# A two-layer decoder's expert layer: experts ranked by token count, the four emptiest with 64 slots and two matmul passes

## The chip, the core and the metric

The kernel runs on one NeuronCore of a Trainium2 chip. The metric is device time in microseconds (us), the median of several runs. The engines are TensorE (PE: matmuls; PEld: its weight loads), VectorE (DVE), ScalarE (ACT), GpSimd (POOL) and SyncE (SP, which here issues the weight transfers). Each engine works through its own list of instructions in order.

## The reference, cut to what matters

256 tokens of width 1024 pass two hybrid layers. Layer 1 ends in a mixture of eight expert SwiGLUs (inner width 2816), each token going to two of them:

```
logits = x @ w_router                       # 256 x 8
top_logit, top_idx = top_k(logits, 2);  top_w = softmax(top_logit)
out[t] = sum over the two experts e of token t:
         top_w * ( (silu(x[t] @ w_gate[e]) * (x[t] @ w_up[e])) @ w_down[e] )
x = layernorm(alpha * x + out)
```

For these inputs experts 0 to 7 get 52, 107, 68, 61, 52, 26, 119 and 27 of the 512 assignments.

## The kernel before, in words

**Weights.** All weights lie in one array `wst` as units of 128 x 2048 float32 (1.05 MB). `fetch` (L178) starts one transfer a unit from SP into a ring of buffers `raw`; in the expert layer one buffer `ga` is part of the ring too. Float32 precision comes from splitting each number: each half unit (128 x 1024) is rounded by ACT to `hi` (L197), and DVE computes `lo = raw - hi` (L199). A product is then three matmuls on 128 x 512 pieces (`mm3`: hi x hi L209, hi x lo L210, lo x hi L211).

**Expert layer** (`moe`). For each expert e, a `gather` (L1004, L1005: matmuls with a one-hot matrix `ohm`) packs its tokens into 128 slots: `xeh` and `xel`, the high and low parts of the packed tokens. Gathers are made for two experts at a time, in steps 3 to 6 of the odd expert before. Then come 11 steps j (`NJ`), 256 inner columns each, with three units a step, six halves (called a to f below; a to d are gate and up, e and f down):

1. gate and up: 24 matmuls into one bank `pa` (128 slots x 256 gate | 256 up);
2. ACT takes silu of the gate half (`fs`, L1095), DVE multiplies by the up half (L1096), PE transposes (L1101), ACT rounds to `hh` (L1105), DVE makes `hl2` (L1106);
3. down: 12 matmuls into two banks `Y`. They are held back (`pend`) and issued amid the gate and up matmuls of step j+1.

After step 10, `scatter` rounds `Y` to `yh` (ACT, L1052) and `yl` (DVE, L1053), brings the rows back to token order by eight matmuls (L1056, L1057), and DVE adds them, weighted, to the sum `ybc` (L222). For an expert this falls into the first steps of the next one.

**Overflow.** `weights`, in step 1 of expert 0, counts tokens per expert and keeps the largest count (`mosti`). `spill`, at expert 4 step 5 (`SPILL`), loads it into a register of every engine (L1121) and branches (`tc.If`, L1136) round a slow path for experts with over 128 tokens. With these inputs the branch is not entered.

The order of instructions on each engine is fixed when the kernel is built: a scheduler places them by the order of the code and by when tiles come free.

Of the kernel before, what the change touches and what calls it, by code (L numbers as in the profile page):

```python
# [45 lines left out]
SPILL = 4, 5  # L46
GA = 3
SPLITS = 3, 4, 3, 2, 3
# [87 lines left out]
class Net:  # L136
# [29 lines left out]
    def fetch(self):  # L166
# [12 lines left out]
        self.unit += 1  # L179
        return raw  # L180
# [21 lines left out]
    def halves(self):  # L202
        raw = self.fetch()
        for h in range(2):
            yield self.split(raw[:, h * 1024:(h + 1) * 1024])
# [708 lines left out]
    def route_consts(self):  # L914
        nc, C = self.nc, self.cst
        self.rt = C.tile([128, 8, NE], F32, name="rt")
        nc.gpsimd.dma_start(self.rt, self.A["router"])
        it = C.tile([128, 128], I32, name="it")
        nc.gpsimd.iota(it, pattern=[[1, 128]], base=0, channel_multiplier=0)
        self.io8 = C.tile([128, NE], F32, name="io8")  # L920
        nc.vector.tensor_copy(self.io8, it[:, 0:NE])
        self.slot = C.tile([128, 128], F32, name="slot")
        nc.vector.tensor_scalar(self.slot, it, 1.0, None, op0=OP.add)
        self.ones = C.tile([128, 128], F32, name="ones")
        nc.vector.memset(self.ones, 1.0)
# [8 lines left out]
        self.xkh = self.xkl = None  # L934

# [27 lines left out]
    def weights(self):  # L963
# [4 lines left out]
        most = C.tile([128, 1], F32, name="most")  # L968
        nc.vector.tensor_reduce(most, ps[:, 0:NE], axis=AX.X, op=OP.max)
        self.most = C.tile([128, 1], I32, name="mosti")  # L970
        nc.vector.tensor_copy(self.most, most)
        ex = C.tile([128, 2, 2], F32, name="ex")
        for m in range(2):
            nc.vector.tensor_scalar(ex[:, m], self.top[:, m, 0:2], self.top[:, m, 0:1], None, op0=OP.subtract)
        nc.scalar.activation(ex, ex, AF.Exp)
        den = C.tile([128, 2], F32, name="den")
        nc.vector.tensor_add(den, ex[:, :, 0], ex[:, :, 1])
        nc.vector.reciprocal(den, den)
        for m in range(2):
            nc.vector.tensor_scalar(ex[:, m], ex[:, m], den[:, m:m + 1], None, op0=OP.mult)  # L980
            nc.vector.tensor_scalar(self.wt[:, m], self.oh8[:, m, 0], ex[:, m, 0:1], None, op0=OP.mult)
            self.stt(self.wt[:, m], self.oh8[:, m, 1], ex[:, m, 1:2], self.wt[:, m])
        self.dump("pos", self.pos)
        self.dump("wt", self.wt)

    def gather(self, es, W):
        nc = self.nc
        n = len(es)
        oh = W.tile([128, 2, n * 128], F32R, name="ohm", bufs=2)
        self.front = []  # L990
        for m in range(2):
            for i, e in enumerate(es):
                self.front.append(nc.vector.tensor_scalar(oh[:, m, i * 128:(i + 1) * 128], self.slot,
                                                          self.pos[:, m, e:e + 1], None, op0=OP.is_equal))
        xeh = [W.tile([128, 8, 128], F32R, name="xeh", bufs=3) for _ in es]
        xel = [W.tile([128, 8, 128], F32R, name="xel", bufs=3) for _ in es]
        for kp in range(4):
            ps = self.pa()
            for kk in range(2):
                k = 2 * kp + kk  # L1000
                s = slice(k * 128, (k + 1) * 128)
                o = ps[:, kk * 256:kk * 256 + n * 128]
                for m in range(2):
                    nc.tensor.matmul(o, lhsT=self.xkh[:, m, s], rhs=oh[:, m], start=m == 0, stop=False)  # L1004
                    nc.tensor.matmul(o, lhsT=self.xkl[:, m, s], rhs=oh[:, m], start=False, stop=m == 1)  # L1005
            pv = ps.rearrange("p (k i t) -> p k i t", k=2, t=128)
            for i in range(n):
                q = slice(2 * kp, 2 * kp + 2)
                nc.scalar.copy(xeh[i][:, q], pv[:, :, i])
                self.front.append(nc.vector.tensor_sub(xel[i][:, q], pv[:, :, i], xeh[i][:, q]))  # L1010
            yield
        return [xeh, xel, oh]
# [8 lines left out]
    def turn(self, oh, W):  # L1021
        nc = self.nc
        oht = W.tile([128, 2, T], F32R, name="oht", bufs=2)
        for i in range(2):
# [5 lines left out]

    def moe(self, W):
        nc = self.nc
        acc = self.macc
        got = coming = None
# [3 lines left out]
        pend = None  # L1038

        def down(j, hh, hl2, wd, Y, ns=(0, 1)):  # L1040
            for f in range(2):
                for n in ns:
                    s = slice(n * 512, (n + 1) * 512)
                    self.mm3(Y[n], hh[:, f], hl2[:, f], wd[f][0][:, s], wd[f][1][:, s], j == 0 and f == 0,
                             j == NJ - 1 and f == 1)

        def scatter(e, Y, oht, ns=(0, 1)):
            for n in ns:
# [5 lines left out]
                for m in range(2):  # L1054
# [3 lines left out]
                    self.stt(acc[:, m, s], ps, self.wt[:, m, e:e + 1], acc[:, m, s])  # L1058

        for e in range(NE):  # L1060
            if e % 2 == 0:
                got = self.finish(coming or self.gather((e, e + 1), W))
                coming = None
                if e == 0:
                    self.after(SPLITS[1], self.front[SPLITS[4]])
            Y = oht = None
            for j in range(NJ):
                if e == 0 and j == 1:
                    self.weights()
# [4 lines left out]
                if e % 2 and e < NE - 1 and GA <= j < GA + 4:  # L1074
                    if coming is None:
                        coming = self.gather((e + 1, e + 2), W)
                    next(coming, None)
                if j == 2:
                    if e % 2 == 0:
                        got[2] = self.turn(got[2], W)  # L1080
                    oht = got[2][:, e % 2]
                ps = self.pa()
                for u in range(2):
                    raw = self.fetch()
                    for h in range(2):
                        hi, lo = self.split(raw[:, h * 1024:(h + 1) * 1024])
                        for kk in range(2):
                            k = 4 * u + 2 * h + kk
                            s = slice(kk * 512, (kk + 1) * 512)
                            self.mm3(ps, got[0][e % 2][:, k], got[1][e % 2][:, k], hi[:, s], lo[:, s], k == 0, k == 7)  # L1090
                        if u == 1 and h == 0 and pend is not None and not (e == NE - 1 and j == NJ - 1):
                            pend()
                            pend = None
                sg = W.tile([128, 256], F32, name="fs", bufs=2)
                nc.scalar.activation(sg, ps[:, 0:256], AF.Silu)  # L1095
                nc.vector.tensor_mul(sg, sg, ps[:, 256:512])  # L1096
                wd = list(self.halves())
                last = e == NE - 1 and j == NJ - 1
                pt = self.pb()
                for f in range(2):  # L1100
                    nc.tensor.transpose(pt[:, f * 128:(f + 1) * 128], sg[:, f * 128:(f + 1) * 128], self.ident)  # L1101
                hh = W.tile([128, 2, 128], F32R, name="hh", bufs=2)
                hl2 = W.tile([128, 2, 128], F32R, name="hl2", bufs=2)
                pv = pt[:, 0:256].rearrange("p (a t) -> p a t", a=2)
                nc.scalar.copy(hh, pv)  # L1105
                nc.vector.tensor_sub(hl2, pv, hh)  # L1106
# [4 lines left out]
                def pend(ns=(0, 1), j=j, hh=hh, hl2=hl2, wd=wd, Y=Y, e=e, oht=oht):  # L1111
                    down(j, hh, hl2, wd, Y, ns)
                    if j == NJ - 1:
                        scatter(e, Y, oht, ns)
        for n in range(2):
            before((n,))
            pend((n,))

    def spill(self, W, base):
# [16 lines left out]
        with tc.If(most > 128):  # L1136
            nc.vector.tensor_scalar(pos, self.pos, -128.0, None, op0=OP.add)
# [134 lines left out]
```

## Time and profile before

| | us |
|---|---|
| median of 3 runs | 1595.93 (1594.56 to 1597.03) |
| span of the profiled execution | 1596.8 |
| PE busy | 1525.8 (96%) |
| DVE busy | 1275.7 (80%) |
| ACT busy | 933.8 (58%) |
| last silu (L1095) starts | 1576.03 |

The profiled execution's own time is its span, 1596.8 us, 0.9 us over the median. Of the span, 0 to about 770 us are the mixers, the dense layer and the router, about 770 to 1586 us the expert layer, and the rest is the last layernorm and the output. A matmul's bar in the trace is longer than the distance to the next one, because matmuls overlap: a 128 x 512 matmul shows 0.40 us, and the next starts 0.23 to 0.24 us later. In a table by stretches the columns are the stretch, its length, the busy time of each engine with the number of its instructions, the granted clock of TensorE (1.00 is full), the busy share of the DMA engines, and GB/s.

### The profile page before, as it was taken

What the parts mean: (1) busy time and instruction counts of PE and PEld (TensorE: products, weight loads), DVE (VectorE), ACT (ScalarE), POOL (GpSimd) and SP (SyncE); (2) the same over time, 40 slices, a digit from 0 to 9 for tenths busy, and PEclk for the clock granted to TensorE, in tenths of its full rate; (3) what the DMA queues carried; (4) which work ended last, traced back from release to release, by engine and by line L of the source; (5) the groups of instructions that cost most, each with busy time, mean ns of one, the idle gap of its engine ahead of it and who ended that gap; (6) DMA issues with size and microseconds to landing.
All of it is one profiled execution on the core that took longest, in us unless ns stands there. A gap on an engine that the chain in (4) does not pass through costs nothing. (4 is left out here: it accounts for less than half of the span.)

```text
span 1596.8 us, 23711 instructions
## 1 busy us (share of the span) xinstructions
PE 1525.8 (96%) x9398; PEld 1316.9 (82%) x9398; DVE 1275.7 (80%) x1717; ACT 933.8 (58%) x1235; POOL 44.3 (3%) x80
## 2 busy tenths in 40 slices
PE   7989999999989989999899999999997999999996
PEld 7989988999979989898787887878875888788785
DVE  6899578655555898578898988888887888888887
ACT  6432454544426432455777777776775777767674
POOL 1020000000000210000000000000000000000000
PEclk9999999999999999999899999999998999999998
DMA  6343236555414333254897998989987988899892
GB/s 228 127 151 120 93 139 244 218 205 185 172 67 148 124 136 111 101 206 194 306 353 316 369 343 309 367 324 344 346 311 269 375 341 328 315 362 362 326 370 86
DMA packets 55636, 390.76 MB, mean 245 GB/s; under 512 B 6192, under 2 KB 6192, under 8 KB 9568
## 3 DMA queue, kind: packets, MB, share of 16 engines
q1 hardware_dynamic: 53136, 381.18, 63.4%
q0 software_dynamic: 2096, 7.49, 1.3%
q8 instruction: 75, 1.23, 0.3%
q10 hardware_dynamic: 288, 0.52, 0.1%
q14 instruction: 41, 0.34, 0.1%
HBM read 387.08 MB, written 2.10 MB: 244 GB/s over the span
## 5 line engine op out<-in xcount | busy, mean ns | idle before, releaser
L199 DVE TENSOR_TENSOR lo<-raw,hi 128x1024 fp32r<-128x1024 f32 x648 | 771.3, 1222 | 156.7 <-ACT hi L197 154.0
L197 ACT CAST hi<-raw 128x1024 fp32r<-128x1024 f32 x648 | 656.9, 1050 | 299.9 <-PE pa L210 185.3
L209 PE MATMUL pa<-xTh,hi 128*128 128x256 f32 x1120 | 325.4, 291 | 7.3 <-ACT xTh L348 7.3
L211 PE MATMUL pa<-xTh,lo 128*128 128x256 f32 x1120 | 323.9, 289 | 7.5 <-DVE lo L199 7.3
L210 PE MATMUL pa<-xTl,hi 128*128 128x256 f32 x1120 | 321.9, 287 | 2.3 <-DVE xTl L349 2.0
L211 PE MATMUL pa<-hi,xel 128*128 128x512 f32 x704 | 283.5, 403 | 0.0
L210 PE MATMUL pa<-lo,xeh 128*128 128x512 f32 x704 | 280.9, 399 | 1.2 <-DVE lo L199 1.2
L209 PE MATMUL pa<-hi,xeh 128*128 128x512 f32 x704 | 281.3, 400 | 0.4 <-ACT oht L1028 0.4
L209 PEld LDWEIGHTS pa<-xTh,hi 128*128 128x128 f32 x1120 | 218.7, 195 | 12.0 <-ACT xTh L348 7.3
L211 PEld LDWEIGHTS pa<-xTh,lo 128*128 128x128 f32 x1120 | 218.8, 196 | 11.5 <-DVE lo L199 10.1
L210 PEld LDWEIGHTS pa<-xTl,hi 128*128 128x128 f32 x1120 | 218.6, 195 | 3.6 <-DVE xTl L349 2.3
L209 PE MATMUL pb<-hi,hh 128*128 128x512 f32 x440 | 175.5, 399 | 8.9 <-PEq L1136 5.9
L210 PE MATMUL pb<-lo,hh 128*128 128x512 f32 x440 | 174.7, 397 | 0.0
L211 PE MATMUL pb<-hi,hl 128*128 128x512 f32 x440 | 173.8, 397 | 0.0
L210 PEld LDWEIGHTS pa<-lo,xeh 128*128 128x128 f32 x704 | 133.4, 190 | 32.1 <-DVE lo L199 1.9
L211 PEld LDWEIGHTS pa<-hi,xel 128*128 128x128 f32 x704 | 133.3, 189 | 29.3
L209 PEld LDWEIGHTS pa<-hi,xeh 128*128 128x128 f32 x704 | 133.4, 189 | 29.2 <-ACT oht L1028 0.6
L1095 ACT ACTIVATE fs<-pa 128x256 f32<-128x256 f32 x88 | 33.8, 384 | 138.4 <-PE pa L211 138.4
L209 PEld LDWEIGHTS pb<-hi,hh 128*128 128x128 f32 x440 | 83.2, 189 | 29.6 <-issue 6.1
L211 PEld LDWEIGHTS pb<-hi,hl 128*128 128x128 f32 x440 | 83.3, 189 | 20.2 <-DVE hl L1106 0.2
L210 PEld LDWEIGHTS pb<-lo,hh 128*128 128x128 f32 x440 | 83.2, 189 | 19.4
L199 DVE TENSOR_TENSOR lo<-ga,hi 128x1024 fp32r<-128x1024 f32 x74 | 88.1, 1219 | 8.0 <-ACT hi L197 7.6
(329 smaller groups left out, 1538.3 us busy)
## 6 DMA issues: line engine op xcount, KB each, us to landing
raw<-in_wst SPq DMA_DIRECT2D x322, 1024.0 KB, 6.2
ga<-in_wst SPq DMA_DIRECT2D x37, 1024.0 KB, 6.8
raw<-in_wst SPq DMA_DIRECT2D x4, 512.0 KB, 5.7
xf<-in_xT SPq DMA_DIRECT2D x2, 512.0 KB, 5.6
raw<-in_lora SPq DMA_DIRECT2D x2, 512.0 KB, 5.7
kk<-in_lnp POOLq DMA_DIRECT2D x2, 512.0 KB, 3.8
v<-in_lnp POOLq DMA_DIRECT2D x2, 512.0 KB, 3.7
xsave<-ga POOLq DMA_DIRECT2D x2, 512.0 KB, 2.9
```

The source lines that it names most:

```text
L197: self.nc.scalar.copy(hi, src)
L199: self.nc.vector.tensor_sub(lo, src, hi)
L209: mm(out, lhsT=lh, rhs=rh, start=start, stop=False)
L210: mm(out, lhsT=lh, rhs=rl, start=False, stop=False)
L211: mm(out, lhsT=ll, rhs=rh, start=False, stop=stop)
L1095: nc.scalar.activation(sg, ps[:, 0:256], AF.Silu)
```

## The change

The eight counts are ranked on the chip; rank 0 is always expert 0 (work on it begins before the counts are known), ranks 1 to 7 follow by falling count. The weight transfers of ranks 1 to 7 take their address from a register of SP. Ranks 0 to 3 run as before with 128 slots. Ranks 4 to 7 get 64 slots. Their packed tokens hold the high parts in columns 0 to 63 and the low parts in columns 64 to 127 of one 128 x 128 operand, so that two passes (`mm2`: times `hi`, times `lo`) do what three did; rows 0 to 63 and 64 to 127 of the result then have to be added. In `hidden_small` ACT copies the gate and up bank to `gu`, four float32 matmuls with `fold` (two identities on top of each other) add the two halves and transpose at once, ACT takes silu, DVE multiplies, and ACT and DVE write the high and low parts of `hh` side by side. Gathers are made for rank groups (0), (1, 2), (3), (4, 5), (6, 7). The branch of `spill` moves behind the last scatter, and its condition is now that any expert has more tokens than its slots (128 or 64).

```
-SPILL = 4, 5
-SPLITS = 3, 4, 3, 2, 3
+SPLITS = 3, 4, 3, 2, 1
+BIG = 4
+GROUPS = (0,), (1, 2), (3,), (4, 5), (6, 7)
+LIMITS = 128, 64
...
-        w = self.A["wst"][self.unit]
+        w = self.A["wst"][self.unit] if src is None else src
...
+    def rank(self, cnt, W):                    # on DVE, small tiles, 128 x 8 or 128 x 64
+        self.stt(key, cnt, float(NE), self.tie)
+        nc.vector.tensor_tensor(sq, key[:, None, :].to_broadcast([128, NE, NE]),
+                                key[:, :, None].to_broadcast([128, NE, NE]), op=OP.is_gt)
+        nc.vector.tensor_reduce(rk, sq, axis=AX.X, op=OP.add)
...
+        self.permute(self.posr, self.pos, W)
...
+    def expert_unit(self, r, j, c):
+        if r == 0:
+            return None
+        if r not in self.who:
+            self.who[r] = self.nc.values_load(self.order[0:1, r:r + 1], engines=(mybir.EngineType.SP,),
+                                              min_val=0, max_val=NE - 1)
+        src = self.A["wst"][bass.ds(self.who[r] * (3 * NJ) + (self.base + 3 * j + c), 1)]
...
+    def mm2(self, out, l, rh, rl, start, stop):
+        self.nc.tensor.matmul(out, lhsT=l, rhs=rh, start=start, stop=False)
+        self.nc.tensor.matmul(out, lhsT=l, rhs=rl, start=False, stop=stop)
...
+        def hidden_small(ps):
+            gu = W.tile([128, 512], F32, name="gu", bufs=2)
+            nc.scalar.copy(gu, ps)
+            pt = self.pb()
+            for f in range(4):
+                nc.tensor.matmul(pt[:, f * 64:(f + 1) * 64], lhsT=gu[:, f * 128:(f + 1) * 128], rhs=self.fold,
+                                 start=True, stop=True)
+            sg = W.tile([128, 2, 64], F32, name="fs", bufs=2)
+            pv = pt[:, 0:256].rearrange("p (a t) -> p a t", a=4)
+            nc.scalar.activation(sg, pv[:, 0:2], AF.Silu)
+            nc.vector.tensor_mul(sg, sg, pv[:, 2:4])
+            hh = W.tile([128, 2, 128], F32R, name="hh", bufs=2)
+            nc.scalar.copy(hh[:, :, 0:64], sg)
+            nc.vector.tensor_sub(hh[:, :, 64:128], sg, hh[:, :, 0:64])
+            return (hh,)
...
-                if (e, j) == SPILL:
-                    self.spill(W, self.unit - 3 * (NJ * e + j))
...
+                hh = (hidden_small if small else hidden_big)(ps)
...
+        self.spill(W, self.base)
...
-        with tc.If(most > 128):
+        with tc.If(most > 0):
```

VectorE, one step of a late expert before. `fs_14324` is this step's activation; `lo_14349` and `lo_14359` are halves a and b of the **next** step.

```order
L199 TENSOR_TENSOR lo_14349<-raw_14345,hi_14347 128x1024
L199 TENSOR_TENSOR lo_14359<-raw_14345,hi_14357 128x1024
L1096 TENSOR_TENSOR fs_14324<-fs_14324,pa_14267 128x256
L199 TENSOR_TENSOR lo_14371<-ga_14367,hi_14369 128x1024
L199 TENSOR_TENSOR lo_14393<-ga_14367,hi_14391 128x1024
L1106 TENSOR_TENSOR hl2_14341<-pb_14337,hh_14340 128x256
```

VectorE, the same place after (a step of rank 5). `fs_13767` is this step's activation, `lo_13754` and `lo_13758` are this step's own down halves e and f, and `lo_13778` is half a of the next step.

```order
L201 TENSOR_TENSOR lo_13754<-raw_13750,hi_13752 128x1024
L201 TENSOR_TENSOR lo_13758<-raw_13750,hi_13756 128x1024
L1165 TENSOR_TENSOR fs_13767<-fs_13767,pb_13762 128x128
L201 TENSOR_TENSOR lo_13778<-raw_13774,hi_13776 128x1024
L1168 TENSOR_TENSOR hh_13770<-fs_13767,hh_13770 128x2x64
L201 TENSOR_TENSOR lo_13786<-raw_13774,hi_13784 128x1024
L201 TENSOR_TENSOR lo_13796<-ga_13792,hi_13794 128x1024
```

Before, two halves of the next step are split ahead of the step's multiply (L1096); after, none is. How many stand ahead is called the step's lead below. The list after has the lead 0 at 32 of the 43 steps that lie between the first and the last gate and up of the four small experts, 1 at seven, 2 or 3 at four.

ScalarE, the same step after: `gu_13760` is the copy of the gate and up bank, `fs_13767` the silu, `hi_13776` half a of the next step.

```order
L1157 COPY gu_13760<-pa_13705 128x512
L1164 ACTIVATE fs_13767<-pb_13762 128x128
L199 CAST hi_13776<-raw_13774 128x1024
L1167 CAST hh_13770<-fs_13767 128x2x64
L199 CAST hi_13784<-raw_13774 128x1024
```

The rounding of the next step's first half stands behind the silu, which reads what PE's fold writes.

TensorE, the same step after: `pa_13705` is the bank of this step, `pa_13773` that of the next.

```order
L1105 MATMUL pa_13705<-hi_13742,xe_12586 128x512
L1106 MATMUL pa_13705<-lo_13744,xe_12586 128x512
L1160 MATMUL pb_13762<-fold_7360,gu_13760 128x64 x4
L1105 MATMUL pa_13773<-hi_13776,xe_12586 128x512
L1106 MATMUL pa_13773<-lo_13778,xe_12586 128x512
L1105 MATMUL pa_13773<-hi_13776,xe_12586 128x512
L1106 MATMUL pa_13773<-lo_13778,xe_12586 128x512
L1105 MATMUL pa_13773<-hi_13784,xe_12586 128x512
L1105 MATMUL pb_13286<-hi_13752,hh_13770 128x512
L1106 MATMUL pb_13286<-lo_13754,hh_13770 128x512
```

Between the step's last gate and up matmul and the next step's first there stand only the four folds; the down matmuls of the step (`hh_13770`) come later, among half b. Before, matmuls of the next step's halves a and b stood ahead of the transposes:

```order
L211 MATMUL pa_14267<-hi_14314,xel_13023 128x512
L209 MATMUL pa_14344<-hi_14347,xeh_13021 128x512
L210 MATMUL pa_14344<-lo_14349,xeh_13021 128x512
L211 MATMUL pa_14344<-hi_14347,xel_13023 128x512
L209 MATMUL pa_14344<-hi_14347,xeh_13021 128x512
L210 MATMUL pa_14344<-lo_14349,xeh_13021 128x512
L211 MATMUL pa_14344<-hi_14347,xel_13023 128x512
L209 MATMUL pa_14344<-hi_14357,xeh_13021 128x512
L210 MATMUL pa_14344<-lo_14359,xeh_13021 128x512
L1101 MATMUL pb_14337<-ident_179,fs_14324 128x128 x2
L211 MATMUL pa_14344<-hi_14357,xel_13023 128x512
```

There ten matmuls on halves a and b, whose splits stand ahead of the multiply, are issued before PE needs what ACT and DVE make of this step.

## Rows read from the trace of the kernel before

**Rows 1.** The page: busy time, share of the span and instructions of each engine.

```profile
PE 1525.8 (96%) x9398; PEld 1316.9 (82%) x9398; DVE 1275.7 (80%) x1717; ACT 933.8 (58%) x1235; POOL 44.3 (3%) x80
```

**Rows 2.** Busy time in a stretch of 90 us in the expert layer.

```profile
1290.00:1380.00 90.00, 90.00 (x413) 73.06 (x413) 79.61 (x89) 64.89 (x87) 0.00 (x0) 1.00 0.88 336
```

**Rows 3.** Groups by line, 840 to 1586 us: out<-in, shapes, xcount | busy us, mean ns | idle before.

```profile
L199 DVE TENSOR_TENSOR lo<-raw,hi 128x1024 fp32r<-128x1024 f32 x406 | 476.1, 1218 | 38.3 <-ACT hi L197 37.6
...
L197 ACT CAST hi<-raw 128x1024 fp32r<-128x1024 f32 x406 | 405.7, 1051 | 40.8 <-PE pb L211 33.5 <-PE pa L211 6.3 <-DVE ohm L993 0.5
...
L211 PE MATMUL pa<-hi,xel 128*128 128x512 f32 x637 | 256.7, 403 | 0.0
...
L1095 ACT ACTIVATE fs<-pa 128x256 f32<-128x256 f32 x80 | 30.7, 384 | 136.0 <-PE pa L211 136.0
...
L222 DVE SCALAR_TENSOR_TENSOR ybc<-pb,wt,ybc 128x512 f32<-128x512 f32 x32 | 21.9, 743 | 3.5 <-PE pb L1057 3.4
...
L1004 PE MATMUL pa<-ohm,xTh 128*128 128x256 f32 x48 | 11.9, 280 | 0.0
```

**Rows 4.** ACT in order of time, one step: start us, us, engine, line [idle <-releaser].

```profile
1552.74 0.38 ACT L1095 ACTIVATE fs<-pa 128x256 f32<-128x256 f32 x1 [2.30 <-PE pa L211]
...
1553.03 1.99 ACT L197 CAST hi<-raw 128x1024 fp32r<-128x1024 f32 x2
...
1561.35 0.39 ACT L1095 ACTIVATE fs<-pa 128x256 f32<-128x256 f32 x1 [2.28 <-PE pa L211]
```

**Rows 5.** PE in order of time, behind two gaps at an expert's start.

```profile
1390.78 0.44 PE L1101 MATMUL pb<-ident,fs 128*128 128x128 f32 x2 [1.17 <-DVE fs L1096]
...
1391.89 0.60 PE L209 MATMUL pb<-hi,hh 128*128 128x512 f32 x1 [0.54 <-ACT hh L1105]
...
1395.28 0.53 PE L211 MATMUL pb<-hi,hl 128*128 128x512 f32 x1
...
1396.34 0.40 PE L210 MATMUL pa<-lo,xeh 128*128 128x512 f32 x1
...
1396.58 0.40 PE L211 MATMUL pa<-hi,xel 128*128 128x512 f32 x1
```

**Rows 6.** ACT: yh of experts 3, 4, 5; first and last silu of experts 4 to 7.

```profile
1171.74 0.59 ACT L1052 CAST yh<-pb 128x512 fp32r<-128x512 f32 x1 [2.09 <-PE pb L211]
...
1175.70 0.39 ACT L1095 ACTIVATE fs<-pa 128x256 f32<-128x256 f32 x1 [0.78 <-PE pa L211]
...
1284.89 0.59 ACT L1052 CAST yh<-pb 128x512 fp32r<-128x512 f32 x1 [2.08 <-PE pb L211]
...
1385.34 0.59 ACT L1052 CAST yh<-pb 128x512 fp32r<-128x512 f32 x1 [2.07 <-PE pb L211]
...
1576.03 0.38 ACT L1095 ACTIVATE fs<-pa 128x256 f32<-128x256 f32 x1 [1.61 <-PE pa L211]
```

**Rows 7.** Waits, 1200 to 1245 us, around the branch of `spill`: total us, times, longest.

```profile
PE pb L209 <- PEq L1136: 5.9, 1, 5.9
...
DVE ohm L993 <- DVEq L1136: 0.9, 1, 0.9
```

**Rows 8.** Groups by line over the whole span: a copy of 128x512, float32 matmuls.

```profile
L1052 ACT CAST yh<-pb 128x512 fp32r<-128x512 f32 x16 | 9.4, 588 | 17.7 <-PE pb L211 16.9
...
L664 PE MATMUL pb<-QR,Sbd 128*128 128x64 f32 x48 | 6.6, 281 | 0.0
```

**Rows 9.** Busy time in four stretches of 10 us with gaps on PE.

```profile
1070.00:1080.00 10.00, 7.98 (x35) 5.95 (x34) 9.59 (x13) 8.34 (x11) 0.00 (x0) 1.00 0.54 192
...
1230.00:1240.00 10.00, 8.34 (x30) 6.17 (x29) 9.79 (x11) 7.73 (x11) 0.00 (x0) 0.83 0.89 330
...
1390.00:1400.00 10.00, 8.67 (x32) 6.88 (x33) 10.00 (x11) 7.06 (x10) 0.00 (x0) 0.83 0.54 202
...
1490.00:1500.00 10.00, 8.04 (x35) 6.23 (x35) 10.00 (x12) 7.24 (x9) 0.00 (x0) 1.00 0.47 180
```

**Rows 10.** Busy time in a stretch ahead of the expert layer.

```profile
710.00:720.00 10.00, 10.00 (x87) 10.00 (x86) 7.15 (x8) 6.26 (x8) 0.00 (x0) 1.00 1.01 425
```

More of the change, by code (lines that the diff above doesn't have):

```diff
@@ L200, in split, with halves @@
         return hi, lo
-    def halves(self):
-        raw = self.fetch()
+    def halves(self, src=None):
+        raw = self.fetch(src)
         for h in range(2):
@@ L986, in gather, with permute @@
+    def permute(self, out, src, W):
+        nc = self.nc
+        t = W.tile([128, 256], F32, name="fs", bufs=2)[:, 0:128].rearrange("p (m a b) -> p m a b", m=2, a=NE)
+        for m in range(2):
+            nc.vector.tensor_mul(t[:, m], self.perm, src[:, m, None, :].to_broadcast([128, NE, NE]))
+        nc.vector.tensor_reduce(out, t, axis=AX.X, op=OP.add)
     def gather(self, es, W):
         nc = self.nc
+        big = es[0] < BIG
+        w = LIMITS[0 if big else 1]
         n = len(es)
-        oh = W.tile([128, 2, n * 128], F32R, name="ohm", bufs=2)
+        pos = self.posr if es[0] else self.pos
+        oh = W.tile([128, 2, 256], F32R, name="ohm", bufs=2)
@@ L1019, in finish, with turn @@
                 return r.value
-    def turn(self, oh, W):
+    def turn(self, oh, n, W):
         nc = self.nc
         oht = W.tile([128, 2, T], F32R, name="oht", bufs=2)
-        for i in range(2):
+        for i in range(n):
             ps = self.psA.tile([128, 512], F32R, name="pa")
@@ L1029, in turn, with gate_up @@
         return oht
+    def expert_unit(self, r, j, c):
[5 more added lines that the diff above has]
+        src = self.A["wst"][bass.ds(self.who[r] * (3 * NJ) + (self.base + 3 * j + c), 1)]
+        return src.rearrange("a p c -> p (a c)")
+    def gate_up(self, xe, halves, ps, k0):
+        for h, (hi, lo) in enumerate(halves):
+            for kk in range(2):
+                k = k0 + 2 * h + kk
+                s = slice(kk * 512, (kk + 1) * 512)
+                if len(xe) == 2:
+                    self.mm3(ps, xe[0][:, k], xe[1][:, k], hi[:, s], lo[:, s], k == 0, k == 7)
+                else:
+                    self.mm2(ps, xe[0][:, k], hi[:, s], lo[:, s], k == 0, k == 7)
+            yield
+    def mm2(self, out, l, rh, rl, start, stop):
+        self.nc.tensor.matmul(out, lhsT=l, rhs=rh, start=start, stop=False)
+        self.nc.tensor.matmul(out, lhsT=l, rhs=rl, start=False, stop=stop)
     def moe(self, W):
@@ L1033, in moe @@
         acc = self.macc
-        got = coming = None
         u, n = self.unit, sum(n for _, n in self.rings)
@@ L1037, in moe, with down @@
         self.cycle = [order[(i - u) % (n + 1)] for i in range(n + 1)]
-        pend = None
-        def down(j, hh, hl2, wd, Y, ns=(0, 1)):
+        self.base, self.who = u, {}
+        pend = coming = got = None
+        place = {r: (g, i) for g, es in enumerate(GROUPS) for i, r in enumerate(es)}
+        def down(j, hh, wd, Y, ns=(0, 1)):
             for f in range(2):
@@ L1057, in scatter, with hidden_big @@
                     nc.tensor.matmul(ps, lhsT=oht[:, m * 128:(m + 1) * 128], rhs=yl, start=False, stop=True)
[L1058 to L1062, printed above, removed]
+                    self.stt(acc[:, m, s], ps, self.wtr[:, m, r:r + 1], acc[:, m, s])
+        def hidden_big(ps):
+            sg = W.tile([128, 256], F32, name="fs", bufs=2)
+            nc.scalar.activation(sg, ps[:, 0:256], AF.Silu)
+            nc.vector.tensor_mul(sg, sg, ps[:, 256:512])
+            pt = self.pb()
+            for f in range(2):
+                nc.tensor.transpose(pt[:, f * 128:(f + 1) * 128], sg[:, f * 128:(f + 1) * 128], self.ident)
+            hh = W.tile([128, 2, 128], F32R, name="hh", bufs=2)
+            hl = W.tile([128, 2, 128], F32R, name="hl2", bufs=2)
+            pv = pt[:, 0:256].rearrange("p (a t) -> p a t", a=2)
+            nc.scalar.copy(hh, pv)
+            nc.vector.tensor_sub(hl, pv, hh)
+            return hh, hl
@@ L1063, in moe @@
+        for r in range(NE):
+            g, i = place[r]
+            if i == 0:
+                got = self.finish(coming or self.gather(GROUPS[g], W))
                 coming = None
-                if e == 0:
+                if r == 0:
                     self.after(SPLITS[1], self.front[SPLITS[4]])
+            xe, small = got[0][i], r >= BIG
+            ahead = GROUPS[g + 1] if i == len(GROUPS[g]) - 1 and r < NE - 1 else None
             Y = oht = None
             for j in range(NJ):
-                if e == 0 and j == 1:
-                    self.weights()
+                if r == 0 and j == 1:
+                    self.weights(W)
@@ L1078, in moe @@
                 if j == 2:
-                    if e % 2 == 0:
-                        got[2] = self.turn(got[2], W)
-                    oht = got[2][:, e % 2]
+                    if i == 0:
+                        got[1] = self.turn(got[1], len(GROUPS[g]), W)
+                    oht = got[1][:, i]
                 ps = self.pa()
                 for u in range(2):
[L1084 to L1091, printed above, removed]
+                    for h, _ in enumerate(self.gate_up(xe, self.halves(self.expert_unit(r, j, u)), ps, 4 * u)):
+                        if u == 1 and h == 0 and pend is not None and not (r == NE - 1 and j == NJ - 1):
@@ L1092, in moe @@
                             pend()
                             pend = None
[L1094 to L1106, printed above, removed]
+                wd = list(self.halves(self.expert_unit(r, j, 2)))
+                hh = (hidden_small if small else hidden_big)(ps)
                 if Y is None:
@@ L1135, in spill @@
         pr = self.psA.tile([128, 512], F32R, name="pa")
-        with tc.If(most > 128):
-            nc.vector.tensor_scalar(pos, self.pos, -128.0, None, op0=OP.add)
+        with tc.If(most > 0):
+            for m in range(2):
+                nc.vector.tensor_sub(pos[:, m], self.pos[:, m], self.cap)
             nc.vector.tensor_copy(wt, self.wt)
```

91 lines of the change are left out of this document (65 added, 26 removed).

## The prediction

> **What bounds the kernel now.** I read the page first. PE is busy 1525.8 of 1596.8 us, DVE 80%, ACT 58% [rows 1]. The reader is to see that PE leads, but that DVE is not far behind. The change touches only the expert layer, so I read that next, by stretches: between two expert starts PE is busy for all of 90 us at full clock, DVE for 79.6, ACT for 64.9, and DMA moves 336 GB/s [rows 2]. There PE alone sets the pace. The groups by line say the same: silu (L1095) waited 136.0 us in total for PE's last gate and up matmul, while PE's own matmuls hardly waited [rows 3]. A step j lasts from one silu to the next, 1552.74 to 1561.35, 8.61 us [rows 4]: 36 matmuls and two short transposes, some 0.235 us a matmul.
>
> So one would say: take a third of PE's matmuls away in half of the experts, and PE has 12 x 0.235 = 2.8 us less a step. The question is what ends a step when PE no longer does. For that I read the order of the lists, as shown with the change, and put the durations of the rows on it.
>
> **Part 1: a small step with lead 0.** Let 0 be the end of the step's last gate and up matmul, and follow who waits for whom.
> - For each hand-over between engines I allow 0.03 to 0.07 us, an estimate; 0.3 in all. ACT starts at 0.07 and copies 128 x 512 to `gu` in 0.59, as the copy of that size does [rows 8]: 0.66.
> - PE has four float32 folds of 128 x 64. A float32 matmul is two records, and 48 such records took 6.6 us [rows 8], so eight take 1.1: from 0.72 to 1.82.
> - ACT takes silu of 128 x 128. The 128 x 256 one took 0.384 [rows 3], the 128 x 512 copy 0.588 [rows 8], so some 0.28: 1.89 to 2.17.
> - Only now comes half a of the next step on ACT's list. ACT starts an instruction about 0.1 before the bar of the one ahead ends (1552.74 + 0.38 against 1553.03 [rows 4]), and a rounding takes 1.05 [rows 3]: 2.08 to 3.13.
> - DVE subtracts, 1.22 [rows 3]: 3.16 to 4.38. The multiply of this step fits ahead of it.
> - PE's first `lo` matmul of half a can go at 4.43. One `hi` matmul went before; 23 of the 24 matmuls of the step are left. They are fed faster than PE takes them (ACT needs 1.05 and DVE 1.22 for a half, PE 4 to 8 matmuls, 0.94 to 1.9 us). 22 x 0.235, 0.10 for the first one after a gap and 0.40 for the last bar make 5.66: **10.1 us**.
>
> Thus the step is 1.5 longer than before, although PE has only 24 x 0.235 + 1.1 = 6.7 us of work in it, DVE six halves of 1.17 (476.1 over 406 [rows 3]) and two short operations, 7.6, ACT 6.8. No engine is full; the time goes round in turn. Before, the ten matmuls ahead of the transposes covered the way over ACT and DVE. After, the folds stand where nothing is ready to cover them.
>
> **Part 2: the other small steps.** With lead 1 one DVE half less is waited for, 10.1 - 1.2 = 8.9. With lead 2 or 3 only PE's work and the 0.7 up to `gu` remain, 7.4. At the three changes between small experts and the four first steps, `yh`, `yl` and the weighted adds lie among the halves; the four adds alone are 3.0 us of DVE at 0.74 each [rows 3], of which I put 1.3 and 1.1 us on the path, 3 x 1.3 + 4 x 1.1 = 8.3 together. Bounds are 0 (hidden in the 2.5 us that DVE has free in a step) and 7 x 3.0 = 21.
> The 43 steps: 32 x 10.1 + 7 x 8.9 + 4 x 7.4 + 8.3 = 423.4 us. Before, from the first silu of expert 4 to the last of expert 7 it was 1576.03 - 1175.70 = 400.3 [rows 6], of which the branch of `spill` takes 12.7: expert 4 needs 1284.89 - 1171.74 = 113.15, expert 5 1385.34 - 1284.89 = 100.45 [rows 6]. Without it 387.6. **Part 2 costs +35.8 us.**
>
> **Part 3: the branch in the middle goes: -12.7 us.** PE waits 5.9 us for its sequencer there, DVE 0.9 [rows 7]; the rest is the restart of the splits and a low clock. Bounds: 5.9 and 12.7; the two experts differ in nothing else that I see, so the upper one.
>
> **Part 4: the branch at the end: +1.5 us.** At the end PE has no work behind it. DVE and ACT have. DVE's wait was 0.9 [rows 7], and one statistics instruction that lay between the adds now stands behind the branch, 0.6. Upper bound: DVE pays what PE paid, 5.9. The last down has four matmuls fewer: -0.8.
>
> **Part 5: ranking and gathers: +2.5 us.** There are five gathers for four. A gather of two experts is 32 matmuls; the 48 of one line took 11.9 us between as many of the other [rows 3], so 32 take about 4. With 128 columns a matmul is bound by its weight load, so the fifth gather costs up to 4 in an expert that PE bounds; the first gather is shorter, which gives back some. Bounds 0 and 4. The ranking is some twenty DVE operations on tiles of 8 to 128 columns in step 1 of expert 0, at most 0.28 each, 5 us; six halves are split ahead there, so I take nothing. If that cover were gone, it would be 5. The transfers with an address from a register add one instruction on SP for each transfer; three transfers in 10 us leave SP idle most of the time: nothing. DMA has to bring 3.15 MB a step, in 10.1 us 311 GB/s, under the 336 it moves now [rows 2]; it doesn't bind.
>
> **Part 6: the clock.** A lead-0 step leaves PE without work, folds and one matmul apart, from 0 to 4.4 us. At an expert's start before, gaps of 1.17 and 0.54 us were followed by eight matmuls at 0.42 us, 1391.89 to 1395.28, against 0.24 later [rows 5], which is the lower level, 1.2 GHz: 1.5 to 1.6 us lost. It doesn't follow each time: of the six stretches of 10 us in the expert layer with PE busy 7.98 to 9.0, apart from the branch, two show a clock of 0.83 and the others 1.00 [rows 9]. A small step has less PE than any of these, 6.7 of 10.1. Bounds: none, and 32 x 1.6 = 51. I take half, **+25.6**.
>
> One page of the Trainium skill bears on this: "TensorE: Matmul & The Clock Gate", section "HAM oscillation — how this bites in real kernels", tells of a kernel whose bursts of matmuls, each shorter than the wait ahead of it, pay the return to full clock in every round. By that, part 6 would be the upper bound. The rows here agree for a third of the gaps.
>
> **Sum.** 1596.8 + 35.8 - 12.7 + 1.5 - 0.8 + 2.5 = 1623.1 at full clock, 1648.7 with half of the clock falls. The profiled execution is 0.9 above the median of its runs, so **1648 us**, 3% slower.
>
> **Rivals.**
> 1. *The small steps run at their work (faster).* If the chain of part 1 doesn't hold, because halves for the next step are ready after all, a step takes DVE's 7.6 us. Then the 43 steps take 43 x 7.6 + 8.3 = 335, and the whole 1596.8 - 52.5 - 9.5 = 1535. For it: every engine has the time, and 425 GB/s was moved ahead of the expert layer [rows 10], where 3.15 MB in 7.6 us asks 414. Against it: the lists are fixed and DVE and ACT can't take half a before the multiply and the silu. It decides the sign from a lead-0 step of 9.3 us on (397.1 us for the 43 steps, which eats up the 9.5 of the other parts), 0.8 less than my chain: about as much as errors in six hand-overs could make if the clock stayed up. Chance 0.18 for 1535 to 1593.
> The Trainium skill, "DMA: Bandwidth & Descriptors", section "Specifications", gives some 358 GB/s from HBM for one core. By that, a step couldn't be under 8.8 us, and this rival would stop at some 1586. The 425 GB/s of [rows 10] speak against it as a limit for one core alone.
> 2. *The clock falls at every lead-0 step.* 1623.1 + 51 - 0.9 = 1673; with the low clock in some others 1685. For it: the gaps are longer than those of [rows 5]. Against: [rows 9], at 1070 and 1490. Chance 0.18 (1660 to 1690).
> 3. *The saving and the waits cancel*, 1593 to 1599: chance 0.04.
> 4. *The overflow branch is entered or costs as on PE.* By the counts ranks 4 to 7 hold 61, 52, 27 and 26 tokens, none over 64, so it isn't entered; with 5.9 for DVE the time is 5 more. Chance 0.02 for more than that.
>
> **Numbers.** The forecast, 1600 to 1660, has 0.58. What can be told from no change is about 0.2%, 3 us. Faster 0.18, same 0.04, slower 0.78. The range, leaving out some 0.17 of rival 1 and 0.03 above: 1590 to 1682.
>
> **What would show it.** Right: in ranks 4 to 7 PE busy under 75%, its idle time ahead of the `lo` matmuls of half a put down to DVE, ACT's silu waiting for the fold and the fold for `gu`, 10 to 12 us from one `gu` to the next, PE's clock below 1.00 in many stretches, the hole at 1214 to 1238 gone, under 2 us of wait at the branch at the end. Wrong: steps under 9.3 us, DVE busy over 85% there, or a clock of 1.00 throughout, which takes 26 us off.

## The result, and the profile after

The changed kernel takes 1684.8 us (median of 4 runs, 1681.5 to 1689.8), the kernel before 1595.2 beside it: ratio 1.0566, 95% interval 1.0542 to 1.0589. It is slower, as forecast, and by more than forecast: +90 us where the sum had +52, and 3 us above the upper end of the range. The profiled execution spans 1688.1 us, 91.3 more than the one before.

The page after, engines and clock in 40 slices:

```profile
PE 1532.9 (91%) x9166; PEld 1304.6 (77%) x9166; DVE 1266.7 (75%) x1746; ACT 949.6 (56%) x1279; POOL 44.3 (3%) x80
...
PEclk9999999999999999998999999999977978878877
```

PE is busy 91% in place of 96% [rows 1], and its clock leaves the full level from the 30th slice on; the small experts begin in the 29th. Busy time by stretches, all four small experts from the first `gu` to the last:

```profile
1184.00:1668.00 484.00, 386.61 (x1445) 289.14 (x1444) 333.64 (x374) 294.83 (x405) 1.05 (x2) 0.83 0.71 269
```

484 us at a mean clock of 0.83, PE busy 80% even so, DVE 69%, 269 GB/s. In [rows 2] PE was busy all the time; here no engine is. Who waited for whom from 1184 to 1680 us (total us, times, longest):

```profile
ACT gu L1157 <- PE pa L1106: 136.2, 43, 4.6
DVE fs L1165 <- ACT fs L1164: 109.8, 31, 4.5
...
ACT fs L1164 <- PE pb L1160: 41.5, 43, 1.3
...
PE pa L1105 <- ACT hi L199: 36.5, 28, 1.4
PE pa L1106 <- DVE lo L201: 33.3, 46, 2.6
DVE lo L201 <- ACT hi L199: 31.6, 43, 1.8
```

The waits go round: ACT's copy waits for PE's last gate and up matmul, silu for PE's folds, DVE's multiply for silu, DVE's subtraction for ACT's rounding, and PE's next matmuls for these halves. One step of the kernel after on ACT, in order of time:

```profile
1402.25 0.59 ACT L1157 COPY gu<-pa 128x512 f32<-128x512 f32 x1 [3.58 <-PE pa L1106]
1404.03 0.28 ACT L1164 ACTIVATE fs<-pb 128x128 f32<-128x128 f32 x1 [1.20 <-PE pb L1160]
1404.20 1.04 ACT L199 CAST hi<-ga 128x1024 fp32r<-128x1024 f32 x1
...
1414.72 0.58 ACT L1157 COPY gu<-pa 128x512 f32<-128x512 f32 x1 [4.55 <-PE pa L1106]
```

and in the same step on DVE:

```profile
1404.34 0.29 DVE L1165 TENSOR_TENSOR fs<-fs,pb 128x128 f32<-128x128 f32 x1 [3.46 <-ACT fs L1164]
1405.27 1.22 DVE L201 TENSOR_TENSOR lo<-ga,hi 128x1024 fp32r<-128x1024 f32 x1 [0.65 <-ACT hi L199]
1406.41 0.28 DVE L1168 TENSOR_TENSOR hh<-fs,hh 128x128 fp32r<-128x128 f32 x1
```

From `gu` at 1402.25 to the next at 1414.72 it is 12.47 us. The way up to the first subtraction is the one forecast, to 0.1 us. The forecast lets `gu` start 0.07 after the end of the last gate and up matmul; so its 0 lies at 1402.18, silu starts at 1.85 (forecast 1.89), the rounding at 2.02 (2.08), the subtraction at 3.09 (3.16). What is new stands on PE, in order of time:

```profile
1402.89 1.10 PE L1160 MATMUL pb<-fold,gu 128*128 128x64 f32 x8 [0.68 <-ACT gu L1157]
1405.29 0.79 PE L1105 MATMUL pa<-hi,xe 128*128 128x512 f32 x1 [1.30 <-ACT hi L199]
1406.55 0.80 PE L1106 MATMUL pa<-lo,xe 128*128 128x512 f32 x1 [0.47 <-DVE lo L201]
1407.14 0.63 PE L1105 MATMUL pa<-hi,xe 128*128 128x512 f32 x1
...
1411.41 0.63 PE L1106 MATMUL pb<-lo,hh 128*128 128x512 f32 x1
...
1412.19 0.39 PE L1106 MATMUL pb<-lo,hh 128*128 128x512 f32 x1
1412.42 0.40 PE L1106 MATMUL pa<-lo,xe 128*128 128x512 f32 x1
```

After the gap the bars are 0.51 to 0.80 long and most of them come 0.43 apart, and only from 1412.19 on they are 0.40 long and 0.23 apart. That is the lower level, 1.2 GHz, for 14 matmuls; in [rows 5] it was eight. The 25 lead-0 steps inside the experts (those that carry the end of an expert left out) took 300.3 us, 12.0 each. They alternate between about 11.4 and 12.45: the low clock falls on fewer matmuls in every other step (seven to nine in place of 13 to 15). All 25 show it, with a mean clock of 0.85 or 0.73. Of all 32 lead-0 steps one kept the full clock, the first of all: 9.91 us.

Two of the forecast's signs came otherwise: the steps run to 12.5 us and more, not 12, and PE is busy 80%, not under 75%, as its bars are longer at the lower clock.

Where the 91.3 us are, from the first `gu` (1184.19), the last `gu` (1667.09) and the span, against the first and last silu in [rows 6]: +8.5 up to the small experts, 482.9 - 400.3 = +82.6 in their 43 steps, +0.2 behind them.

### The profile page after: what moved, and what is told of

Read it like the earlier page. It is cut to its first block, busy times and chain, and to the rows that moved or that the text cites. A ratio compares the mean times of both kernels' runs of the same rounds, so it can differ in the third digit from the quotient of the medians.

```text
span 1688.1 us, 23779 instructions
## 1 busy us (share of the span) xinstructions
PE 1532.9 (91%) x9166; PEld 1304.6 (77%) x9166; DVE 1266.7 (75%) x1746; ACT 949.6 (56%) x1279; POOL 44.3 (3%) x80
## 5 line engine op out<-in xcount | busy, mean ns | idle before, releaser
L1105 PE MATMUL pa<-hi,xe 128*128 128x512 f32 x352 | 170.5, 484 | 36.5 <-ACT hi L199 36.5
L1106 PE MATMUL pa<-lo,xe 128*128 128x512 f32 x352 | 172.6, 490 | 33.6 <-DVE lo L201 33.3
L211 PE MATMUL pa<-hi,xe 128*128 128x512 f32 x352 | 142.9, 406 | 0.5 <-ACT oht L1081 0.5
L213 PE MATMUL pa<-hi,xe 128*128 128x512 f32 x352 | 142.1, 404 | 0.0
L212 PE MATMUL pa<-lo,xe 128*128 128x512 f32 x352 | 141.6, 402 | 0.0
L1106 PEld LDWEIGHTS pa<-lo,xe 128*128 128x128 f32 x352 | 81.7, 232 | 70.1 <-DVE lo L201 51.7
L1105 PEld LDWEIGHTS pa<-hi,xe 128*128 128x128 f32 x352 | 83.5, 237 | 56.2 <-ACT hi L199 40.4
L211 PE MATMUL pb<-hi,hh 128*128 128x512 f32 x264 | 105.0, 398 | 1.6 <-ACT hh L1151 1.6
L212 PE MATMUL pb<-lo,hh 128*128 128x512 f32 x264 | 104.6, 396 | 0.0
L213 PE MATMUL pb<-hi,hl 128*128 128x512 f32 x264 | 103.3, 396 | 0.0
L1157 ACT COPY gu<-pa 128x512 f32<-128x512 f32 x44 | 25.7, 585 | 136.2 <-PE pa L1106 136.2
L1165 DVE TENSOR_TENSOR fs<-fs,pb 128x128 f32<-128x128 f32 x44 | 12.5, 285 | 109.8 <-ACT fs L1164 109.8
L1105 PE MATMUL pb<-hi,hh 128*128 128x512 f32 x176 | 82.2, 467 | 1.3 <-DVE hh L1168 1.3
```

The costliest lines, as they stand in the source:

```text
L211: mm(out, lhsT=lh, rhs=rh, start=start, stop=False)
L212: mm(out, lhsT=lh, rhs=rl, start=False, stop=False)
L213: mm(out, lhsT=ll, rhs=rh, start=False, stop=stop)
L1105: self.nc.tensor.matmul(out, lhsT=l, rhs=rh, start=start, stop=False)
L1106: self.nc.tensor.matmul(out, lhsT=l, rhs=rl, start=False, stop=stop)
L1157: nc.scalar.copy(gu, ps)
```

## The experiments

Each ratio is to the kernel before, run beside it.

**1. The clock alone.** Behind each fold 20 matmuls whose product is not used keep PE at work; the lead-0 steps are held at lead 0.

```
...
+            for _ in range(20):
+                nc.tensor.matmul(ps[:, 0:256], lhsT=self.identr, rhs=self.xkh[:, 0, 0:256], start=True, stop=True)
...
+                if small and (j == 0 or j >= LEAD0[r]):
+                    self.after(0, self.last_mul)      # next splits are placed behind these two
+                    self.after(0, self.last_silu)
```

> The changed kernel with 20 further matmuls (128 x 256, product not used) on PE behind each fold, so that PE has work while the way over silu, rounding and subtraction is walked; the steps that had lead 0 are held at lead 0. Theory (the clock falls in the gap, and that is all that the steps lose beyond the chain of 10.05 us that the one lead-0 step at full clock showed): PE's clock stays near 1.00 in ranks 4 to 7, lead-0 steps take 10.0 to 10.3 us in place of 11.4 and 12.45, and the whole 1625 to 1635 us. Rival (the longer steps come from something else that goes with two passes, such as transfers with an address from a register): steps stay at 11.4 to 12.5, 1680 to 1690. Rival (the further matmuls themselves get in the way): over 10.5 us a step at full clock, over 1645.

Measured: 1632.8 us (ratio 1.0239, 1.0215 to 1.0263). Busy time over the same stretch of small experts:

```profile
1184.00:1610.00 426.00, 400.53 (x2251) 332.82 (x2249) 324.95 (x364) 289.00 (x395) 1.05 (x2) 1.00 0.79 302
```

The clock is 1.00, and the same 25 lead-0 steps take 250.7 us, 10.03 each: the forecast's 10.1. One of them, PE's rows ahead, then ACT's:

```profile
1469.58 2.62 PE L1165 MATMUL pa<-xTh,identr 128*128 128x256 f32 x20
...
1472.34 0.50 PE L1108 MATMUL pa<-lo,xe 128*128 128x512 f32 x1
...
1468.03 0.59 ACT L1159 COPY gu<-pa 128x512 f32<-128x512 f32 x1 [2.05 <-PE pa L1108]
...
1478.01 0.59 ACT L1159 COPY gu<-pa 128x512 f32<-128x512 f32 x1 [2.05 <-PE pa L1108]
```

With 0 at 1467.96 (`gu` less 0.07) the first `lo` matmul starts at 4.38, the forecast's 4.43, so the further matmuls don't hold it up. So the chain is right, and the clock is what it lacks: 49.6 us in these 25 steps, 2.0 each, and 58 with the seven lead-0 steps at expert ends and starts. More work on PE made the kernel 52 us faster, since the further matmuls lie in time in which PE waited anyway. The 52 are not the clock alone: in the profiled executions the other 11 steps took 9.5 us longer than after, and the small experts began 9.2 us earlier.

**2. The branch and the ranking alone.** The kernel before with the branch moved to the end; and the changed kernel with all ranks big (`BIG = 8`).

```
-                if (e, j) == SPILL:
-                    self.spill(W, self.unit - 3 * (NJ * e + j))
...
+        self.spill(W, u)
```

> The kernel before, with the branch of spill moved behind the last scatter and nothing else. Theory: the 12.7 us of expert 4 go, under 1 us comes at the end, 1583 to 1585 us. Rival (the branch's time returns elsewhere, in waits for transfers that it hid): 1590 or more.

> The changed kernel with all eight ranks run as the four big ones (128 slots, three passes): what is left of the change is the ranking, the addresses from a register, the five gathers and the branch at the end. Theory: as the kernel with only the branch moved, plus 4 us for the fifth gather and 1 to 3 us at the expert starts: 1588 to 1592. Rival (ranking or addresses cost much of the loss): over 1600.

Measured: 1586.1 us with the branch at the end (ratio 0.9942, 0.9924 to 0.9960), 1598.0 with all ranks big (1.0018, 1.0005 to 1.0032). The branch moved is worth 8.5 us in the medians and 10.9 in the spans, and the time lies 1 us over the range expected. At the end it costs 0.15 us, from the last add to the first statistics, as DVE shows in order of time:

```profile
1572.68 1.41 DVE L221 SCALAR_TENSOR_TENSOR ybc<-pb,wt,ybc 128x512 f32<-128x512 f32 x2 [0.59 <-PE pb L1056]
1574.24 1.88 DVE L844 BATCH_NORM_STATS2 st<-ybc 128x6 f32<-128x512 f32 x3
```

1572.68 + 1.41 = 1574.09 against 1574.24. The second kernel lies 12 us over the first, not 4 to 7. Its trace puts 3.8 on the four steps with the fifth gather (9.55 in place of 8.62), some 3 on three expert starts of 11.54 in place of 10.49, 1.9 on the stretch ahead of the expert layer, whose lists are the same but for three short DVE instructions at 15 us (more on this at the end), and the rest on one more expert start with a low clock (12.6, 12.9). Neither the ranking's DVE operations nor the addresses from a register show as a wait. The medians say so much: branch, ranking and gathers together are about +3 us, so nearly all of the +90 (87 by the medians) is the small experts.

**3. Lead 2.** The next step's first unit is fetched and split before `hidden_small`, all else as in the change.

```
...
+                if r >= BIG and (r, j) != (NE - 1, NJ - 1):
+                    ready = list(self.halves(self.expert_unit(*((r, j + 1) if j < NJ - 1 else (r + 1, 0)), 0)))
                 hh = (hidden_small if small else hidden_big)(ps)
```

> The changed kernel with one move in the code: in ranks 4 to 7 the first unit of the next step is fetched and split before the step's activation is made, so that the lists hold two halves of the next step ahead of it (lead 2). Passes, folds, gu, slots and the branch at the end are as in the change. Theory (lead 0 is the cause): the steps take 7.9 to 8.2 us, as the lead-2 steps of the changed kernel do (8.1), the clock stays near 1.00, and the whole is 1550 to 1565 us, faster than before. Rival (the copy to gu and the fold are the cost, wherever the halves stand): the steps stay over 9 us, 1610 or more. Rival (transfers limit small steps at 358 GB/s, 8.8 us a step): some 1587.

Measured: 1606.2 us (ratio 1.0076, 1.0052 to 1.0100): 79 us better than the change, but not faster than before, and 41 over the range expected. Most steps take 9.1 us at full clock or 10.05 at a mean clock of 0.83; the clock fell in 17 of 43 steps. One step of this kernel on ACT, in order of time:

```profile
1335.13 0.58 ACT L1157 COPY gu<-pa 128x512 f32<-128x512 f32 x1 [1.82 <-PE pa L1106]
1335.61 2.00 ACT L199 CAST hi<-raw 128x1024 fp32r<-128x1024 f32 x2
1337.51 0.27 ACT L1164 ACTIVATE fs<-pb 128x128 f32<-128x128 f32 x1
```

and on DVE:

```profile
1336.69 2.36 DVE L201 TENSOR_TENSOR lo<-raw,hi 128x1024 fp32r<-128x1024 f32 x2 [1.75 <-ACT hi L199]
```

The two halves stand ahead of silu, but behind `gu` (1335.13), and so they still wait for the end of the step. I had counted the lead at DVE's multiply; on ACT, the instruction that waits first is the copy. The first rival, that the copy and the folds cost this much wherever the halves stand, fits these steps as well; experiment 4 decides between the two.

**4. Lead 2 ahead of `gu`, and lead 4.** The copy is placed behind the rounding of half b; in the second kernel all four halves are split ahead.

```
...
+            with self.tc.issue_after(self.last_hi.ins):
                 nc.scalar.copy(gu, ps)
...
+                    ready = [list(self.halves(self.expert_unit(*q, c))) for c in range(2)]   # second kernel only
```

> The kernel with lead 2 (e2), and ACT's copy to gu held behind the rounding of the next step's halves a and b. In e2 these two stood ahead of silu and of DVE's multiply but behind gu, so they still waited for the end of the step. Theory (a half that waits for gu is as good as not ahead; the way gu, rounding, subtraction, 23 matmuls is what e2 still pays, 0.66 + 0.95 + 1.25 + 5.7 = 8.6 and a clock that falls): steps of 7.6 to 8.0 us, which is DVE's work, clock 1.00, the whole 1545 to 1558 us. Rival (transfers at 358 GB/s, 8.8 us a step): 1580 to 1590 and DVE waiting for transfers. Rival (clock and gaps stay for another reason): as e2, 1600 to 1610.

> As e5, with all four gate and up halves of the next step split ahead (lead 4 in place of 2). Theory (DVE's work of 7.6 us a step is the bound once the lead is there, so more lead gives nothing): within 0.4% of e5. Rival (two halves are too little because PE needs c and d early): 0.5% or more faster than e5. Rival (the multiply behind four subtractions makes hh late for the down matmuls, and the fetches run out of buffers): 0.5% or more slower than e5.

Measured: 1576.4 us (ratio 0.9889, 0.9863 to 0.9915) and 1579.8 (0.9908, 0.9882 to 0.9934). Both are faster than the kernel before, by about 1%, and 0.2% apart, as expected of a longer lead. So the copy and the folds are not the cost wherever the halves stand. The clock is 1.00 but for one step in each, but the steps are 8.65 in both, 0.65 over the theory. 3.15 MB in 8.65 us is 364 GB/s, which looked like the transfers. The rows of the first of the two in order of time, DVE ahead, say otherwise:

```profile
1521.69 1.23 DVE L201 TENSOR_TENSOR lo<-raw,hi 128x1024 fp32r<-128x1024 f32 x1 [0.65 <-ACT hi L199]
...
1523.04 5.76 DVE L201 TENSOR_TENSOR lo<-raw,hi 128x1024 fp32r<-128x1024 f32 x5
1529.40 0.29 DVE L1166 TENSOR_TENSOR fs<-fs,pb 128x128 f32<-128x128 f32 x1 [0.60 <-ACT fs L1165]
1530.34 1.23 DVE L201 TENSOR_TENSOR lo<-raw,hi 128x1024 fp32r<-128x1024 f32 x1 [0.65 <-ACT hi L199]
```

and PE, around the folds:

```profile
1527.72 0.50 PE L1106 MATMUL pa<-lo,xe 128*128 128x512 f32 x1 [0.74 <-DVE lo L201]
1528.05 1.00 PE L1161 MATMUL pb<-fold,gu 128*128 128x64 f32 x8
```

DVE subtracts without a pause for 5.76 us, so no transfer is late. But PE has a `lo` matmul of the next step ahead of the folds; it waits for the fourth of those subtractions (1527.72), the folds for it (1528.05), then silu, the rounding and DVE's next subtraction (1530.34) for them. From 1521.69 to 1530.34 that is a closed round of 8.65. With four halves ahead it is of the same kind: there the last `lo` matmul ahead of the folds is one of half b (1525.59, folds at 1525.93, silu at 1526.96).

**5. The folds first.** PE's matmuls of the next step are placed behind the folds.

```
...
+                    with self.tc.issue_after(self.folded.ins):
                         self.mm2(ps, xe[0][:, k], hi[:, s], lo[:, s], k == 0, k == 7)
```

> As e5, and on PE the first matmuls of the next step are held behind the folds of this one. In e5 one lo matmul of the next half a stood ahead of the folds; it waits for DVE, and with it the folds, silu, the next rounding and the next subtraction: 8.65 us a step, which the rows give as one closed round with DVE idle 1.25 in it. Theory (that round is what e5 and e6 still pay, not the transfers): steps of 7.4 to 7.9 us, DVE over 93% busy, over 400 GB/s, the whole 1530 to 1548 us. Rival (transfers: 3.15 MB in 8.65 us is 364 GB/s, near the page's 358): steps stay at 8.6 to 8.8, 1572 to 1585. Rival (the first matmuls ahead of the folds covered the way over gu): steps of 8.0 to 8.5.

Measured: 1560.1 us (ratio 0.9779, 0.9761 to 0.9798), steps 8.11. The round is opened, and the transfers were not the limit; but 8.11 is over the 7.9 of the theory, and 1560 over its 1548: within the third case's 8.0 to 8.5. The cause is not that case's: DVE still stops once a step, for the rounding of half c behind silu (DVE in order of time):

```profile
1508.78 0.29 DVE L1169 TENSOR_TENSOR fs<-fs,pb 128x128 f32<-128x128 f32 x1
1509.71 1.23 DVE L201 TENSOR_TENSOR lo<-raw,hi 128x1024 fp32r<-128x1024 f32 x1 [0.65 <-ACT hi L199]
...
1516.89 0.29 DVE L1169 TENSOR_TENSOR fs<-fs,pb 128x128 f32<-128x128 f32 x1
```

**6. Three halves ahead.** As 5, with half c rounded ahead of `gu` too.

```
-                    ready = list(self.halves(...))
...
+                    ready = [list(self.halves(self.expert_unit(*q, 0)))]
+                    rest = self.halves(self.expert_unit(*q, 1))
+                    ready.append(chain([next(rest)], rest))
```

> As e7, with three halves of the next step rounded ahead of gu in place of two. In e7 DVE still idles 0.65 us a step, for half c's rounding, which stands behind silu. Theory (that is the last wait in the round): steps of 7.4 to 7.6 us, DVE over 97% busy, 415 GB/s or more, the whole 1530 to 1542 us. Rival (transfers become the bound below 8.1 us a step): steps of 7.8 to 8.1 and ACT or DVE waiting for transfers, 1550 to 1560. Rival (the fetches run out of buffers with a third half ahead): 8.1 us or more, 1560 or more.

Measured: 1544.2 us (ratio 0.9687, 0.9658 to 0.9717), 140 us better than the change and 51 better than before, the best of all. Busy time in a late stretch:

```profile
1440.00:1510.00 70.00, 63.90 (x298) 48.83 (x296) 69.54 (x79) 62.28 (x84) 0.27 (x1) 1.00 0.97 395
```

DVE is busy 69.5 of 70 us, steps are 7.0 to 7.8. Now it is an engine that bounds the small experts, DVE. The 395 GB/s that come in are under the 415 expected, and the DMA engines are busy 97%; [rows 10] had 425 GB/s, so there is little left behind DVE. The whole is 2 us over the expected range: rank 5's four steps with a gather take 9.4, one of them 10.9 at a mean clock of 0.84.

**7. Lead 0 with three passes.** The kernel of 2 with the branch at the end, and in experts 4 to 7 the next splits held behind silu and the multiply; the step's own down halves are split ahead of silu, as in the change.

```
...
+                if e >= 4:
+                    self.after(0, silu)
+                    self.after(0, mul)
```

> The kernel before with the branch at the end (e3: three passes, 128 slots, no ranking), and in experts 4 to 7 the splits of the next step held behind silu and the multiply, as the change has them: lead 0 with everything else as before. Theory (lead 0 is the cause, with two passes or three): step = 0.45 to silu, rounding to 1.4, subtraction to 2.65, 35 matmuls = 11.4 us at full clock against 8.62, and clock falls on top: 1700 to 1770 us. Rival (lead 0 matters only beside gu and the folds; PE has the transposes and more matmuls in between): steps under 9.3 us, under 1615.

Measured once: 1651.8 us. The steps take 10.27 us, less than the theory's 11.4, and more than its rival's 9.3. Busy time in most of these experts:

```profile
1184.00:1610.00 426.00, 387.54 (x1604) 289.20 (x1602) 324.32 (x349) 264.83 (x341) 0.00 (x0) 1.00 0.78 300
```

The clock stayed at 1.00 but for the start of the last expert. I had counted 35 matmuls behind the first subtraction; four down matmuls go ahead of it (PE in order of time):

```profile
1502.43 0.40 PE L210 MATMUL pa<-hi,xel 128*128 128x512 f32 x1
1503.75 0.44 PE L1101 MATMUL pb<-ident,fs 128*128 128x128 f32 x2 [0.93 <-DVE fs L1094]
1504.23 0.50 PE L208 MATMUL pa<-hi,xeh 128*128 128x512 f32 x1
1504.65 0.50 PE L208 MATMUL pb<-hi,hh 128*128 128x512 f32 x1
...
1505.46 0.39 PE L209 MATMUL pb<-lo,hh 128*128 128x512 f32 x1
1505.69 0.39 PE L209 MATMUL pa<-lo,xeh 128*128 128x512 f32 x1
```

The same step on ACT:

```profile
1502.86 0.38 ACT L1093 ACTIVATE fs<-pa 128x256 f32<-128x256 f32 x1 [3.79 <-PE pa L210]
...
1504.23 0.37 ACT L1105 CAST hh<-pb 128x256 fp32r<-128x256 f32 x1
...
1513.13 0.38 ACT L1093 ACTIVATE fs<-pa 128x256 f32<-128x256 f32 x1 [3.79 <-PE pa L210]
```

With three passes `hh` holds the high part alone and is whole once ACT has written it (1504.23), so these four can start at 1504.65. In a two-pass step DVE writes the second half of `hh`, behind the subtraction (1406.41 in the step of the change above). So lead 0 costs a three-pass step 1.65 us, from 8.62 to 10.27. A two-pass step with lead 0 takes 10.03 at full clock: the third of the matmuls that it does without saves 0.24 us. PE's gap is 0.93 us here, and the clock stays; in the change PE has only the folds for 3.1 us, and the clock falls. Passes, folds and slots differ at once between the two, so which of them makes the low clock is not shown.

## Why the prediction was right and wrong

- **Part 1, the chain of a lead-0 step: right.** 10.1 forecast, 10.03 at full clock (experiment 1), and hand-over by hand-over in the rows after. One clause is too simple: a half with four matmuls keeps PE for 0.94 us, less than DVE's 1.22. In the step shown under experiment 1 no wait came of it. Experiments 3 to 6 show the same from the other side: opening the round piece by piece gives 1606, 1576, 1560, 1544 with the same passes, folds and slots.
- **Part 2: right in size.** With lead 1 the steps took 9.0 to 9.3 but for one of 10.0 (8.9 forecast), with lead 2 or 3 8.1 and 7.4 (7.4). These 11 steps are 4.3 us over the sum. The 32 lead-0 steps with the expert starts come to 328.7 at full clock (experiment 1), 331.5 forecast.
- **Part 3, -12.7: a little too much.** Moving the branch alone is worth 8.5 to 10.9 us, and that 12.7 came so near is partly luck. Experts 4 and 5 do differ: expert 5 holds a gather, four steps of 9.56 in place of 8.62, and its first step took 8.61 us where it takes 11.05 with the branch at the end. Step by step the branch cost 14.0 us in expert 4 and gave 2.5 back in expert 5.
- **Part 4, +1.5 - 0.8: too much by 0.5.** DVE pays 0.15 at the end where it paid 0.9 in the middle.
- **Part 5, +2.5: too low.** The small experts began 8.5 later. The gather is at its upper bound, 3.8; two expert starts of 12.5 and 12.6 in place of 11.6 and 11.1, both with a clock of 0.86, and 1.7 us ahead of the expert layer, were not in the sum.
- **Part 6, the clock, "I take half, +25.6": this is the step that failed.** The mechanism is the one named, the size is not. The clock fell at all 25 lead-0 steps inside the experts, not at half of them, and cost 2.0 on average, not 1.6: 58 us with the expert starts and ends, 32 more than in the sum. I let the six stretches of [rows 9] vote, although the same paragraph says that a small step has less PE than any of them, and although one of the two with a low clock, at 1230, still lies in the hole of the branch; and the price came from a gap of 1.7 us in all [rows 5], while the steps have 3.1 us up to the first 512-column matmul. 1623.1 + 58 + 4 (part 2, the other 11 steps) + 6 (part 5) - 3 (the 32 steps at full clock) is 1688, the span. Rival 2 (1660 to 1690), given 0.18, is what came.
- **Rival 1 (faster)** didn't come, for the reason given against it. Its time was within reach, though: it put 1535 on steps of 7.6 us, and experiment 6 has some 7.4 a step and 1544.
- **The two pages of the Trainium skill.** By the page "TensorE: Matmul & The Clock Gate" of the Trainium skill, section "HAM oscillation — how this bites in real kernels", every round would pay for the return to full clock; here all 25 steps did, at 0.83 over 484 us, though the matmuls of a step take over 8 us and the wait ahead of them 3.1. The 358 GB/s of the Trainium skill's "DMA: Bandwidth & Descriptors", section "Specifications", is no limit for one core here: 395 GB/s over 70 us in experiment 6.

## What to carry to other kernels

When work is taken from the engine that bounds, read the order of the lists before the sum of the work: the next wait is often a round over several engines, none of them full, and it has to be opened at each instruction that waits for the end of the step (here `gu`, the folds, silu), one after the other. An instruction "ahead of" one wait may still stand behind another. And if TensorE gets a gap in every step, price the clock too: in the change it fell in all 25 steps with 3.1 us of folds and waiting, in experiment 3, whose usual gaps are 0.67 us ahead of the folds and 0.76 behind, in 17 of 43, and in experiment 7, with a gap of 0.93, in none inside the experts. What the clock costs can be tried by itself with matmuls whose product is not used.

## What was not expected of the hardware

The stretch ahead of the expert layer has the same instruction lists in the kernels after, 1, 3 to 6 and in the one with all ranks big, yet the router's first matmul started at 745.4, 745.9, 746.9, 749.9, 750.6 and 752.0 us in them. The granted clock differs there: 0.91 after and 1.00 in experiment 3, from 120 to 160 us. The busy time in that stretch, after:

```profile
120.00:160.00 40.00, 38.88 (x478) 37.45 (x476) 35.13 (x66) 10.24 (x16) 0.55 (x1) 0.91 0.35 121
```

and in experiment 3:

```profile
120.00:160.00 40.00, 38.89 (x507) 37.30 (x506) 37.23 (x70) 11.57 (x18) 0.54 (x1) 1.00 0.35 120
```

So a difference under some 7 us (0.4%) between two profiled executions need not come from the edit. Nor does it take another program: 17 runs of the kernel before, beside experiments 1 to 3, went from 1589.8 us at a mean clock of 0.983 to 1601.0 at 0.976. The medians of several runs tell finer differences than one profile does. Why the clock fell in one and not in the other was not tried. Nor was it tried why the lead-0 steps alternate between 11.4 and 12.45.
